# Attention of a hybrid decoder trunk: masked choice, maximum and exponential taken in the accumulator bank, sink added apart, two groups' outputs joined, keys split wider

## The chip, the cores and the metric

The kernel runs on one core of one Trainium2 chip. The metric is the device time of one execution, in microseconds (us). The kernel before takes 2112.53 us, the median of three runs between 2110.27 and 2112.72. The core has a TensorE (PE, matmuls; its weight loads are listed as PEld), a VectorE (DVE), a ScalarE (ACT), a GpSimd (POOL), a SyncE (SP) that issues the transfers here, and eight accumulator banks (PSUM) of 128 partitions by 512 fp32 values that the matmuls write.

## The reference

A trunk of two layers over 1024 tokens of width 1024. Layer 0 mixes tokens by a causal convolution module. Layer 1 mixes them by attention over a sliding window of 128 tokens, with 16 query heads, 4 key and value heads (groups of 4 heads share one), and one learned sink per head, all from one K and V computed at the start of layer 1. After each mixer come a layer norm, a squared-ReLU MLP, a second layer norm and a gated embedding.

What the change touches is the attention:

```
def swa_sink_attention(x, w_q, sinks, w_o, kk, vv, cos, sin):
    q = partial_rope((x @ w_q).reshape(B, T, N_HEADS, HEAD_DIM), cos, sin)
    scores = jnp.einsum("bnqkgd,bnskd->bnkgqs", q, kk) * (1.0 / math.sqrt(HEAD_DIM))
    scores = jnp.where(mask, scores, -jnp.inf)
    lse = jnp.logaddexp(jax.nn.logsumexp(scores, axis=-1, keepdims=True), sink)
    probs = jnp.exp(scores - lse).astype(vv.dtype)
    out = jnp.einsum("bnkgqs,bnskd->bnqkgd", probs, vv)
    return out.reshape(B, T, N_HEADS * HEAD_DIM) @ w_o
```

The queries are taken in 8 blocks of 128. A block sees 256 keys (the previous block and its own), of which the mask leaves 128 for each query: key s of the own block if s is not later than the query, else key s of the previous block. So for each query and each s from 0 to 127 exactly one of two scores counts, and the kernel chooses it (the masked choice). The first block has no previous one.

## The kernel before, in words

**How it is written and ordered.** The program does not write instructions for the engines directly. It notes them, with the tiles that they read and write, in a recorder; a planner (`schedule`) then lays all of them out in time with a cost for each operation, always taking the ready operation that comes first in program order, and issues each engine's instructions in the order that it found. On the chip each engine works through its own list in that order and waits at each instruction for what it needs. Because PE has matmuls of independent work in its list (the projection of later queries, for one), the planner can place those where attention's own matmuls are not ready yet. All instructions are issued from one line (L485), so the profile tells them apart by tile names.

**Tiles and slots.** Each kind of tile has a number of slots (`SLOTS`) that are given out in program order: `ps` 6 accumulator banks and `tr` 2, `t` 5 work tiles of 128x512, `z` 4, `g` 4, `X`, `A`, `B`, `E` for larger stores, and so on. `move(a, b)` takes one slot of kind a when it is free and makes it one of kind b. The trace names a slot by its first kind, so a bank called `ps` or `tr` in a row may serve as `sc` or `pv`. A dependency on a bank is on the whole bank, for readers too: two instructions that use one bank come one after the other.

**fp32 from two halves.** An fp32 operand is split into a high half (ACT copies it, rounded) and a rest (DVE subtracts): `split`. A product then takes three matmuls (high x high, high x rest, rest x high).

**Attention, keys and values** (`attention`). The K and V projection runs for tokens 512 to 1023 and then for 0 to 511, four blocks at a time, each block in its own bank. For each block, ACT copies V out, `rope` turns K, PE transposes K's two 128x128 pieces, and for each of the four groups ACT writes the scaled high half and DVE the rest, 64x128 each, into `kT` (64 partitions of high halves above 64 of rests, so that one matmul contracts both). Two key blocks that lie in different halves are copied side by side into `k34`.

**Attention, queries.** Then `sc` gets two of the banks and `pv` one. For gp = 0 and 1 (two groups each) and n = 0 to 7 (query blocks): 24 matmuls of 512 columns project one block's 8 heads into one `ps` bank; `rope` turns them (ACT copies, DVE multiplies and adds); POOL lays each head down twice (for the two halves of `kT`). For each of the two groups `scores` is called, and `values` for the group that came two before it.

- `scores`: 4 transposes and a split give the queries. For each pair of heads, 4 matmuls of 256 columns (128 for n = 0) fill a bank `sc`; ACT copies the previous block's scores to the SBUF tile `s`, and DVE's copy_predicated puts the own block's scores over them where the mask says so. A column of `s` beside the 128 holds the sink, put there by POOL. Once both pairs are in, one DVE reduce over 4 x 129 gives the negated maxima, four ACT exponentials over 129 columns give the weights and their sums with the sink's own term in it, DVE takes the reciprocals, and POOL scales the four heads.
- `values`: 4 transposes of the weights, a split, masked copies by POOL, and 4 matmuls of 512 columns (2 for n = 0) into the bank `pv`, whose upper 64 partitions hold the sum's second part. Heads stand in pairs: for the even and the odd heads apart, ACT copies 64x256 and DVE adds 64x256, into a tile of 128x256; a split into the final tiles follows for each group.

Where the result of group gp goes is fixed: gp = 0 into `att`, gp = 1 into the `xT` tiles that the output projection (`mix_out`) reads as its left operand.

Of the kernel before, what the change touches and what calls it, by code (L numbers as in the profile page):

```python
# [10 lines left out]
F32 = mybir.dt.float32  # L11
F32R = mybir.dt.float32r
AF = mybir.ActivationFunctionType
ALU = mybir.AluOpType
# [503 lines left out]
class Emit:  # L518
# [1383 lines left out]
    def attention(self):  # L1902
# [5 lines left out]
        o = 256 + NT * 32  # L1908
        self.sink = ac[:, o : o + NH]
        nc.sync.dma_start(self.sink, d["sinks"].to_broadcast([P, NH]))  # L1910
        self.products, self.turned = nc.tile("zz", (P, 1024)), 0

        kT = {(g, p): self.sb("B", F32R) for p in range(2) for g in range(4)}
# [8 lines left out]
        for tg in (range(4, 8), range(0, 4)):  # L1922
            nc.slack = WORK_SLACK
            for k in range(4 if tg[0] else 0):
                self.work("w_o", k, "X")
            nc.slack = 0.0
            for ps, t in zip(self.tok_group(tg, us, each=2), tg):
                nc.scalar.copy(vf[t // 2][:, t % 2 * 256 : (t % 2 + 1) * 256], ps[:, 256:512])
                kf = self.sb("t")[:, 0:256]
                self.rope(ps[:, 0:256], kf, t, 4)  # L1930

                pt = self.transpose4([kf[:, j * P : (j + 1) * P] for j in range(2)])
                cols = slice(t % 4 * P, (t % 4 + 1) * P)
                for g in range(4):
                    hi, lo = (kT[g, t // 4][r, cols] for r in ROWS)
                    src = pt[ROWS[g % 2], g // 2 * P : (g // 2 + 1) * P]
                    nc.scalar.activation(hi, src, AF.Identity, scale=HD ** -0.5)
                    nc.vector.scalar_tensor_tensor(
                        out=lo, in0=src, scalar=HD ** -0.5, in1=hi.bitcast(F32), op0=ALU.mult, op1=ALU.subtract
                    )  # L1940
                if t in (3, 4):
                    for g in range(4):
                        nc.scalar.copy(k34[:, g, t - 3, :], kT[g, t // 4][:, cols].bitcast(F32))
        ws.done(4)
        self.kT, self.k34 = kT, k34

        for a, b in (("ps", "sc"), ("ps", "sc"), ("ps", "pv"), ("bo", "v"), ("bo", "v"), ("z", "v")):
            nc.move(a, b)
        att = [self.pair("XE"[t // 4], F32R) for t in range(NT)]
        pend = []  # L1950
        for gp in range(2):
            us = ws.get(4)
            for n in range(NT):
                ps = self.tok_group([n], us)[0]

                q1 = self.sb("t")
                self.rope(ps, q1, n, 8)
                qf = [self.sb("t") for gl in range(2)]
                for gl in range(2):
                    src = q1[:, gl * 256 : (gl + 1) * 256].rearrange("p (h e) -> p h e", e=HD)  # L1960
                    nc.gpsimd.tensor_copy(
                        qf[gl].rearrange("p (h r e) -> p h r e", r=2, e=HD), src.unsqueeze(2).to_broadcast([P, 4, 2, HD])
                    )

                col = n % 2 * 256 + gp * P
                own = vf[n // 2][:, col : col + P].rearrange("p (g e) -> p g e", g=2)
                if n == 0:
                    vd = [self.value_forms(own, q1 if gp == 0 else None)]
                else:
                    if n > 1:  # L1970
                        vd = [self.value_forms(last, q1 if n < 3 and gp == 0 else None)]
                    df = self.sb("t")[:, 0:P].rearrange("p (g e) -> p g e", g=2)
                    nc.vector.tensor_tensor(out=df, in0=own, in1=last, op=ALU.subtract)
                    vd = [vd[0], self.value_forms(df, q1 if n < 3 and gp == 0 else None)]
                last = own
                for gl in range(2):
                    if gp == 0:
                        dst = [a.rearrange("p (k t) -> p k t", k=4)[:, 2 * gl : 2 * gl + 2, :] for a in att[n]]
                    else:
                        dst = [x[:, 2 * gl : 2 * gl + 2, n % 4 * P : (n % 4 + 1) * P] for x in self.xT[1, n // 4]]  # L1980
                    p = self.scores(n, 2 * gp + gl, qf[gl])
                    pend.append((p, gl, vd, dst))
                    if len(pend) > 2:
                        self.values(*pend.pop(0))
            ws.done(4)
        for p in pend:
            self.values(*p)
        nc.move("mid", "raw")
        for a, b in (("ps", "sc"), ("ps", "sc"), ("ps", "pv"), ("bo", "v"), ("bo", "v"), ("z", "v")):
            nc.move(b, a)  # L1990

        self.x = []
# [24 lines left out]
    def scores(self, n, g, qf):  # L2017

        nc = self.nc
        nb = min(n, 1) + 1  # L2020
        hs = slice(4 * g, 4 * g + 4)
        pq = self.transpose4(self.blocks(qf))
        qT = [self.sb("g", F32R) for j in range(2)]
        self.split(pq, *qT)
        sm = self.small(16)
        nm, su = (sm[:, 4 * i : 4 * i + 4] for i in range(2))
        if n == 4:
            ks = self.k34[:, g].rearrange("p b t -> p (b t)")
        else:
            o = (n % 4 + 1 - nb) * P  # L2030
            ks = self.kT[g, n // 4][:, o : o + nb * P]

        s = nc.tile("z", (P, 4 * SC)).rearrange("p (h s) -> p h s", h=4)
        with nc.after(qf) if n == 0 else contextlib.nullcontext():
            nc.gpsimd.tensor_copy(s[:, :, P], self.sink[:, hs])
            if n == 0:
                nc.gpsimd.memset(s[:, :, 0:P], NEG)
        for jj in range(2):
            ps = self.ps("sc").rearrange("p (a b) -> p a b", a=2)
            for j in range(2):  # L2040
                qs = slice((2 * jj + j) * P, (2 * jj + j + 1) * P)
                nc.tensor.matmul(ps[:, j, 0 : nb * P], qT[0][:, qs], ks, start=True, stop=False)
                nc.tensor.matmul(ps[:, j, 0 : nb * P], qT[1][:, qs], ks, start=False, stop=True)
            dst = s[:, 2 * jj : 2 * jj + 2, 0:P]
            if n:
                nc.scalar.copy(dst, ps[:, :, 0:P])
            nc.vector.copy_predicated(
                out=dst, mask=self.own.bitcast(mybir.dt.int32).unsqueeze(1).to_broadcast([P, 2, P]),
                data=ps[:, :, (nb - 1) * P : nb * P],
            )  # L2050
        nc.vector.reduce_max(out=nm, in_=s[:, :, 0 : P + 1], axis=mybir.AxisListType.X, negate=True)
        for h in range(4):
            nc.scalar.activation(
                s[:, h, 0 : P + 1], s[:, h, 0 : P + 1], AF.Exp, bias=nm[:, h : h + 1], scale=1.0,
                accum_out=su[:, h : h + 1],
            )
        nc.vector.reciprocal(su, su)
        for h in range(4):
            nc.gpsimd.tensor_scalar(
                out=s[:, h, 0:P], in0=s[:, h, 0:P], scalar1=su[:, h : h + 1], scalar2=0.0,  # L2060
                op0=ALU.mult, op1=ALU.add,
            )
        return s

    def values(self, s, gl, vd, dst):

        nc = self.nc
        pp = self.transpose4([s[:, h, 0:P] for h in range(4)])
        tr = []
        for k, v in enumerate(vd):  # L2070
            pT = [self.sb("A", F32R) for j in range(2)]
            if k == 0:
                self.split(pp, *pT)
                full = pT
            else:
                for a, b in zip(pT, full):
                    self.own_keys(a, b)
            v = v[:, gl].rearrange("p s e -> p (s e)")
            tr += [(v[:, 0:P], pT[0]), (v[:, HD : HD + P], pT[1])]
        po = self.ps("pv")  # L2080
        for i, (l, r) in enumerate(tr):
            nc.tensor.matmul(po, l, r, start=i == 0, stop=i == len(tr) - 1)
        pv = po.rearrange("p (a e t) -> p a e t", a=2, e=2)
        o = self.sb("t")[:, 0:256].rearrange("p (a t) -> p a t", a=2)
        for e in range(2):
            r = slice(e * HD, (e + 1) * HD)
            nc.scalar.copy(o[r], pv[0:HD, :, e, :])
            nc.vector.tensor_tensor(out=o[r], in0=o[r], in1=pv[HD:P, :, e, :], op=ALU.add)
        self.split(o, *dst)

    def own_keys(self, dst, src):

# [60 lines left out]
def layout(a):  # L2153
    c = np.ascontiguousarray

    def tokmov(w):
        k = w.shape[0] // P
        n = w.shape[1] // HT
        return c(w.reshape(k // 2, 2, P, n, HT).transpose(3, 0, 2, 1, 4).reshape(n, k // 2, P, 1024))
# [58 lines left out]
    r["w_o"] = tokmov(np.asarray(a["attn_w_o"])[0])  # L2218
# [23 lines left out]
```

## Time and profile before

| what | value |
|---|---|
| median of the runs (lowest, highest) | 2112.53 us (2110.27, 2112.72) |
| span of the profiled execution, first to last instruction | 2106.6 us |
| PE busy over the span | 2094.4 us (99%), 9912 matmuls |
| DVE, ACT, POOL busy over the span | 1724.8, 1232.9, 320.7 us |
| in the 150 us from 1150 to 1300 (the query loop): PE, DVE, ACT, POOL busy | 149.86, 130.56, 131.78, 97.25 us |

The profiled execution's own time is known by its span, 2106.6 us; the runs are timed from outside it and stand 5.9 us above (2112.53 less 2106.6), for what lies before the first and behind the last instruction. A row of a group reads: line, engine, operation, output tile and inputs, shapes, count, then busy time and the mean duration of one in ns, then the time that the engine stood idle just before these and what ended it. The K and V projection lies from about 1100 to 1131 us, the query loop from there to about 1315.

### The profile page before, as it was taken

What the parts mean: (1) busy time and instruction counts of PE and PEld (TensorE: products, weight loads), DVE (VectorE), ACT (ScalarE), POOL (GpSimd) and SP (SyncE); (2) the same over time, 40 slices, a digit from 0 to 9 for tenths busy, and PEclk for the clock granted to TensorE, in tenths of its full rate; (3) what the DMA queues carried; (4) which work ended last, traced back from release to release, by engine and by line L of the source; (5) the groups of instructions that cost most, each with busy time, mean ns of one, the idle gap of its engine ahead of it and who ended that gap; (6) DMA issues with size and microseconds to landing.
All of it is one profiled execution on the core that took longest, in us unless ns stands there. A gap on an engine that the chain in (4) does not pass through costs nothing.

```text
span 2106.6 us, 29589 instructions
## 1 busy us (share of the span) xinstructions
PE 2094.4 (99%) x9912; PEld 1742.3 (83%) x9912; DVE 1724.8 (82%) x2724; ACT 1232.9 (59%) x2326; POOL 320.7 (15%) x548
## 2 busy tenths in 40 slices
PE   9999999999999999999999999999999999999999
PEld 7888888888888888888888888888888888888877
DVE  8999789987876879877976888699787778888688
ACT  6776754766655533345656988367666663333374
POOL 0533114000000000002121666140000000000040
PEclk9999999999999999999999999999999999999999
DMA  6669954788786757564486113677878786575635
GB/s 225 196 203 294 302 188 155 279 270 289 255 286 209 264 174 242 187 196 150 172 308 225 61 41 117 223 235 257 277 257 283 256 284 198 180 245 168 237 117 198
DMA packets 215385, 458.51 MB, mean 218 GB/s; under 512 B 21824, under 2 KB 52288, under 8 KB 215232
## 3 DMA queue, kind: packets, MB, share of 16 engines
q1 hardware_dynamic: 215232, 456.62, 64.7%
q8 instruction: 78, 1.28, 0.2%
q14 instruction: 75, 0.61, 0.1%
HBM read 311.04 MB, written 145.49 MB: 217 GB/s over the span
## 4 chain that ended last, share of the span: by engine, by line
PE 93%; DMA 2%; DVE 2%; ACT 1%; issue 1%; POOL 1%; SPq 0%; DVEq 0%; POOLq 0%; ACTq 0%
PE ps L485 73%; PE tr L485 20%; ACT z L485 1%; POOL sm L485 1%; DMA wh<-gate_t 0%; DMA gate_low_t<-xh 0%; DMA form<-t 0%; DVE g L485 0%; DMA z<-in_w_dw_dram 0%; DMA gate_low_b<-xl 0%; DVE t L485 0%; DVE z L485 0%; SPq L485 0%; DMA X<-in_xT_dram 0%; DMA wl<-form 0%
## 5 line engine op out<-in xcount | busy, mean ns | idle before, releaser
L485 PE MATMUL ps<-xh 128*128 128x512 f32 x636 | 247.4, 389 | 0.0
L485 PE MATMUL ps<-xl,xh 128*128 128x512 f32 x636 | 247.4, 389 | 0.0
L485 PE MATMUL ps<-xh,xl 128*128 128x512 f32 x636 | 247.4, 389 | 0.0
L485 POOL TENSOR_SCALAR sm<-sm 128x1 f32<-128x1 f32 x72 | 27.1, 378 | 1371.4 <-DVE E L485 607.3
L485 PE MATMUL ps<-xh,wl 128*128 128x512 f32 x472 | 184.5, 391 | 0.1
L485 PE MATMUL ps<-xl,wh 128*128 128x512 f32 x472 | 184.2, 391 | 0.2 <-DVE xl L485 0.2
L485 PE MATMUL ps<-xh,wh 128*128 128x512 f32 x472 | 183.6, 391 | 0.0
L485 ACT CAST wh<-raw 128x1024 fp32r<-128x1024 f32 (+2 forms) x134 | 120.0, 897 | 88.1 <-PE ps L485 60.7
L485 PE MATMUL ps<-wh,xh 128*128 128x512 f32 x404 | 160.5, 399 | 3.5 <-DMA wh<-gate_t 1.2
L485 PE MATMUL ps<-wl,xh 128*128 128x512 f32 x404 | 161.0, 399 | 0.0
L485 PE MATMUL ps<-wh,xl 128*128 128x512 f32 x404 | 160.8, 398 | 0.0
L485 ACT CAST xh<-wh 128x1024 fp32r<-128x1024 f32 x76 | 79.7, 1049 | 119.6 <-PE ps L485 74.1
L485 PEld LDWEIGHTS ps<-xl,xh 128*128 128x128 f32 x636 | 119.4, 188 | 24.9
L485 PEld LDWEIGHTS ps<-xh,xl 128*128 128x128 f32 x636 | 119.4, 188 | 24.7
L485 PEld LDWEIGHTS ps<-xh 128*128 128x128 f32 x636 | 119.4, 188 | 24.6
L485 DVE TENSOR_TENSOR wl<-raw,wh 128x1024 fp32r<-128x1024 f32 (+2 forms) x100 | 98.1, 982 | 48.1 <-ACT wh L485 43.7
L485 ACT CAST wh<-g 128x512 fp32r<-128x512 f32 x136 | 81.3, 619 | 96.0 <-PE ps L485 59.1
L485 DVE TENSOR_TENSOR wl<-g,wh 128x512 fp32r<-128x512 f32 x136 | 91.1, 691 | 41.6 <-ACT wh L485 41.5
L485 DVE TENSOR_TENSOR xl<-wh,xh 128x1024 fp32r<-128x1024 f32 x76 | 92.8, 1221 | 19.0 <-ACT xh L485 18.7
L485 ACT ACTIVATE t<-t 128x512 f32<-128x512 f32 x144 | 91.1, 632 | 26.0 <-DVE t L485 24.3
L485 PEld LDWEIGHTS ps<-xh,wh 128*128 128x128 f32 x472 | 89.0, 188 | 18.5 <-ACT xh L485 0.4
L485 PEld LDWEIGHTS ps<-xl,wh 128*128 128x128 f32 x472 | 88.6, 188 | 18.8 <-DVE xl L485 0.9
(442 smaller groups left out, 5732.0 us busy)
## 6 DMA issues: line engine op xcount, KB each, us to landing
wh<-hid SPq DMA_DIRECT2D x78, 512.0 KB, 4.2
raw<-in_w_up_dram SPq DMA_DIRECT2D x68, 512.0 KB, 4.3
wl<-in_w_down_dram SPq DMA_DIRECT2D x58, 512.0 KB, 4.9
hid<-zz SPq DMA_DIRECT2D x96, 256.0 KB, 4.6
hid<-t SPq DMA_DIRECT2D x64, 256.0 KB, 4.6
z<-in_w_dw_dram SPq DMA_DIRECT2D x56, 288.0 KB, 4.0
raw<-hid SPq DMA_DIRECT2D x30, 512.0 KB, 4.0
hid<-z SPq DMA_DIRECT2D x36, 256.0 KB, 4.8
```

The source lines that it names most:

```text
L485: getattr(getattr(nc, o.eng), o.name)(*a, **k)
```

## The change

In `attention`:

- A second small tile `less` holds the negated sinks, made by one POOL instruction.
- For keys, four blocks are turned first, each into a half of a `t` tile. Then, for each of the two pieces, four transposes fill one bank, and ACT and DVE split 64x512 at a time (all four blocks of a group at once). The copies into `k34` stand behind it.
- `sc` gets three banks, so `ps` is left with two.
- The tiles that a result goes to are chosen for two groups at a time.

In `scores`:

- The scores stay in the bank. For n = 0, DVE first fills the previous block's place in the bank with a large negative number; the matmuls always write the last columns. copy_predicated chooses within the bank, a DVE reduce over 2 x 128 takes the maxima of the pair in the bank, a small DVE instruction negates them and takes the minimum with `less`, and two ACT exponentials read the bank and write `s`. This is done for each pair of heads.
- The sink's term is worked out apart, for the four heads: POOL adds sink and negated maximum, ACT takes the exponential, POOL adds it to the sums.
- ACT's copy, the sink column, POOL's fill for n = 0 and the 129th column are gone.

In `values`:

- The result of a group is one ACT copy 64x512 and one DVE add 64x512, into the lower 64 partitions of a `t` tile for the first and the upper 64 for the second group; one split of 128x512 follows for both. The order of heads that this gives is met by a change of the rows of `w_o` in `layout`, outside the timed program.

```diff
+        self.less = ac[:, o + NH : o + 2 * NH]
+        nc.gpsimd.tensor_scalar(out=self.less, in0=self.sink, scalar1=-1.0, scalar2=0.0, op0=ALU.mult, op1=ALU.add)
...
+            turned = []
             for ps, t in zip(self.tok_group(tg, us, each=2), tg):
                 nc.scalar.copy(vf[t // 2][:, t % 2 * 256 : (t % 2 + 1) * 256], ps[:, 256:512])
-                kf = self.sb("t")[:, 0:256]
-                self.rope(ps[:, 0:256], kf, t, 4)
...
-                        out=lo, in0=src, scalar=HD ** -0.5, in1=hi.bitcast(F32), op0=ALU.mult, op1=ALU.subtract
...
+                if t % 2 == 0:
+                    kf = self.sb("t")
+                turned.append(kf[:, t % 2 * 256 : (t % 2 + 1) * 256])
+                self.rope(ps[:, 0:256], turned[-1], t, 4)
+            h = tg[0] // 4
+            for j in range(2):
+                pt = self.transpose4([v[:, j * P : (j + 1) * P] for v in turned])
+                for e in range(2):
+                    hi, lo = (kT[2 * j + e, h][r] for r in ROWS)
+                    nc.scalar.activation(hi, pt[ROWS[e]], AF.Identity, scale=HD ** -0.5)
                     nc.vector.scalar_tensor_tensor(
+                        out=lo, in0=pt[ROWS[e]], scalar=HD ** -0.5, in1=hi.bitcast(F32), op0=ALU.mult, op1=ALU.subtract
                     )
...
-        for a, b in (("ps", "sc"), ("ps", "sc"), ("ps", "pv"), ("bo", "v"), ("bo", "v"), ("z", "v")):
+        for a, b in (("ps", "sc"), ("ps", "sc"), ("ps", "sc"), ("ps", "pv"), ("bo", "v"), ("bo", "v"), ("z", "v")):
...
-        nm, su = (sm[:, 4 * i : 4 * i + 4] for i in range(2))
+        nm, su, ex = (sm[:, 4 * i : 4 * i + 4] for i in range(3))
...
-        with nc.after(qf) if n == 0 else contextlib.nullcontext():
-            nc.gpsimd.tensor_copy(s[:, :, P], self.sink[:, hs])
-            if n == 0:
-                nc.gpsimd.memset(s[:, :, 0:P], NEG)
         for jj in range(2):
+            pair = slice(2 * jj, 2 * jj + 2)
             ps = self.ps("sc").rearrange("p (a b) -> p a b", a=2)
+            if n == 0:
+                nc.vector.memset(ps[:, :, 0:P], NEG)
             for j in range(2):
                 qs = slice((2 * jj + j) * P, (2 * jj + j + 1) * P)
-                nc.tensor.matmul(ps[:, j, 0 : nb * P], qT[0][:, qs], ks, start=True, stop=False)
-                nc.tensor.matmul(ps[:, j, 0 : nb * P], qT[1][:, qs], ks, start=False, stop=True)
-            dst = s[:, 2 * jj : 2 * jj + 2, 0:P]
-            if n:
-                nc.scalar.copy(dst, ps[:, :, 0:P])
+                to = ps[:, j, (2 - nb) * P : 2 * P]
+                nc.tensor.matmul(to, qT[0][:, qs], ks, start=True, stop=False)
+                nc.tensor.matmul(to, qT[1][:, qs], ks, start=False, stop=True)
+            both = ps[:, :, 0:P]
             nc.vector.copy_predicated(
...
-        nc.vector.reduce_max(out=nm, in_=s[:, :, 0 : P + 1], axis=mybir.AxisListType.X, negate=True)
-        for h in range(4):
-            nc.scalar.activation(
-                s[:, h, 0 : P + 1], s[:, h, 0 : P + 1], AF.Exp, bias=nm[:, h : h + 1], scale=1.0,
...
+            nc.vector.reduce_max(out=ex[:, pair], in_=both, axis=mybir.AxisListType.X)
+            nc.vector.scalar_tensor_tensor(
+                out=nm[:, pair], in0=ex[:, pair], scalar=-1.0, in1=self.less[:, 4 * g + 2 * jj : 4 * g + 2 * jj + 2],
+                op0=ALU.mult, op1=ALU.min,
             )
+            for h in range(2 * jj, 2 * jj + 2):
+                nc.scalar.activation(
+                    s[:, h], ps[:, h - 2 * jj, 0:P], AF.Exp, bias=nm[:, h : h + 1], scale=1.0,
+                    accum_out=su[:, h : h + 1],
+                )
+        nc.gpsimd.tensor_tensor(out=ex, in0=nm, in1=self.sink[:, hs], op=ALU.add)
+        nc.scalar.activation(ex, ex, AF.Exp)
+        nc.gpsimd.tensor_tensor(out=su, in0=su, in1=ex, op=ALU.add)
         nc.vector.reciprocal(su, su)
...
-        pv = po.rearrange("p (a e t) -> p a e t", a=2, e=2)
-        o = self.sb("t")[:, 0:256].rearrange("p (a t) -> p a t", a=2)
-        for e in range(2):
-            r = slice(e * HD, (e + 1) * HD)
-            nc.scalar.copy(o[r], pv[0:HD, :, e, :])
-            nc.vector.tensor_tensor(out=o[r], in0=o[r], in1=pv[HD:P, :, e, :], op=ALU.add)
-        self.split(o, *dst)
+        if gl == 0:
+            self.joint = self.sb("t")
+        o = self.joint
+        r = ROWS[gl]
+        nc.scalar.copy(o[r], po[0:HD])
+        nc.vector.tensor_tensor(out=o[r], in0=o[r], in1=po[HD:P], op=ALU.add)
+        if gl == 1:
+            self.split(o.rearrange("p (k t) -> p k t", k=4), *dst)
```

More of the change, by code (lines that the diff above doesn't have):

```diff
@@ L1926, in attention @@
             nc.slack = 0.0
+            turned = []
             for ps, t in zip(self.tok_group(tg, us, each=2), tg):
                 nc.scalar.copy(vf[t // 2][:, t % 2 * 256 : (t % 2 + 1) * 256], ps[:, 256:512])
-                kf = self.sb("t")[:, 0:256]
-                self.rope(ps[:, 0:256], kf, t, 4)
[L1932 to L1937, printed above, removed]
+                if t % 2 == 0:
[8 more added lines that the diff above has]
+                    nc.scalar.activation(hi, pt[ROWS[e]], AF.Identity, scale=HD ** -0.5)
                     nc.vector.scalar_tensor_tensor(
-                        out=lo, in0=src, scalar=HD ** -0.5, in1=hi.bitcast(F32), op0=ALU.mult, op1=ALU.subtract
+                        out=lo, in0=pt[ROWS[e]], scalar=HD ** -0.5, in1=hi.bitcast(F32), op0=ALU.mult, op1=ALU.subtract
                     )
-                if t in (3, 4):
-                    for g in range(4):
-                        nc.scalar.copy(k34[:, g, t - 3, :], kT[g, t // 4][:, cols].bitcast(F32))
+            for g in range(4):
+                cols = slice(0, P) if h else slice(3 * P, 4 * P)
+                nc.scalar.copy(k34[:, g, h, :], kT[g, h][:, cols].bitcast(F32))
         ws.done(4)
         self.kT, self.k34 = kT, k34
-        for a, b in (("ps", "sc"), ("ps", "sc"), ("ps", "pv"), ("bo", "v"), ("bo", "v"), ("z", "v")):
+        for a, b in (("ps", "sc"), ("ps", "sc"), ("ps", "sc"), ("ps", "pv"), ("bo", "v"), ("bo", "v"), ("z", "v")):
             nc.move(a, b)
@@ L1975, in attention @@
                 last = own
+                if gp == 0:
+                    dst = [a.rearrange("p (k t) -> p k t", k=4) for a in att[n]]
+                else:
+                    dst = [x[:, :, n % 4 * P : (n % 4 + 1) * P] for x in self.xT[1, n // 4]]
                 for gl in range(2):
[L1977 to L1980, printed above, removed]
                     p = self.scores(n, 2 * gp + gl, qf[gl])
@@ L1988, in attention @@
         nc.move("mid", "raw")
-        for a, b in (("ps", "sc"), ("ps", "sc"), ("ps", "pv"), ("bo", "v"), ("bo", "v"), ("z", "v")):
+        for a, b in (("ps", "sc"), ("ps", "sc"), ("ps", "sc"), ("ps", "pv"), ("bo", "v"), ("bo", "v"), ("z", "v")):
             nc.move(b, a)
@@ L2031, in scores @@
             ks = self.kT[g, n // 4][:, o : o + nb * P]
-        s = nc.tile("z", (P, 4 * SC)).rearrange("p (h s) -> p h s", h=4)
-        with nc.after(qf) if n == 0 else contextlib.nullcontext():
-            nc.gpsimd.tensor_copy(s[:, :, P], self.sink[:, hs])
+        s = nc.tile("z", (P, 4 * SC))[:, 0 : 4 * P].rearrange("p (h s) -> p h s", h=4)
+        for jj in range(2):
+            pair = slice(2 * jj, 2 * jj + 2)
+            ps = self.ps("sc").rearrange("p (a b) -> p a b", a=2)
             if n == 0:
-                nc.gpsimd.memset(s[:, :, 0:P], NEG)
@@ L2038, in scores @@
-        for jj in range(2):
-            ps = self.ps("sc").rearrange("p (a b) -> p a b", a=2)
+                nc.vector.memset(ps[:, :, 0:P], NEG)
             for j in range(2):
                 qs = slice((2 * jj + j) * P, (2 * jj + j + 1) * P)
-                nc.tensor.matmul(ps[:, j, 0 : nb * P], qT[0][:, qs], ks, start=True, stop=False)
-                nc.tensor.matmul(ps[:, j, 0 : nb * P], qT[1][:, qs], ks, start=False, stop=True)
-            dst = s[:, 2 * jj : 2 * jj + 2, 0:P]
-            if n:
-                nc.scalar.copy(dst, ps[:, :, 0:P])
+                to = ps[:, j, (2 - nb) * P : 2 * P]
@@ L2047, in scores @@
+                nc.tensor.matmul(to, qT[0][:, qs], ks, start=True, stop=False)
+                nc.tensor.matmul(to, qT[1][:, qs], ks, start=False, stop=True)
+            both = ps[:, :, 0:P]
             nc.vector.copy_predicated(
-                out=dst, mask=self.own.bitcast(mybir.dt.int32).unsqueeze(1).to_broadcast([P, 2, P]),
-                data=ps[:, :, (nb - 1) * P : nb * P],
-            )
-        nc.vector.reduce_max(out=nm, in_=s[:, :, 0 : P + 1], axis=mybir.AxisListType.X, negate=True)
@@ L2052, in scores @@
-        for h in range(4):
-            nc.scalar.activation(
-                s[:, h, 0 : P + 1], s[:, h, 0 : P + 1], AF.Exp, bias=nm[:, h : h + 1], scale=1.0,
-                accum_out=su[:, h : h + 1],
-            )
+                out=both, mask=self.own.bitcast(mybir.dt.int32).unsqueeze(1).to_broadcast([P, 2, P]),
+                data=ps[:, :, P : 2 * P],
+            )
+            nc.vector.reduce_max(out=ex[:, pair], in_=both, axis=mybir.AxisListType.X)
+            nc.vector.scalar_tensor_tensor(
+                out=nm[:, pair], in0=ex[:, pair], scalar=-1.0, in1=self.less[:, 4 * g + 2 * jj : 4 * g + 2 * jj + 2],
+                op0=ALU.mult, op1=ALU.min,
+            )
@@ L2059, in scores @@
             nc.gpsimd.tensor_scalar(
-                out=s[:, h, 0:P], in0=s[:, h, 0:P], scalar1=su[:, h : h + 1], scalar2=0.0,
+                out=s[:, h], in0=s[:, h], scalar1=su[:, h : h + 1], scalar2=0.0,
                 op0=ALU.mult, op1=ALU.add,
@@ L2217, in layout @@
     r["w_q"] = tokmov(np.asarray(a["attn_w_q"])[0])
-    r["w_o"] = tokmov(np.asarray(a["attn_w_o"])[0])
+    heads = np.arange(NH).reshape(2, 2, 4).transpose(0, 2, 1)
+    rows = (heads[..., None] * HD + np.arange(HD)).ravel()
+    r["w_o"] = tokmov(np.asarray(a["attn_w_o"])[0][rows])
     r["sinks"] = c(np.asarray(a["attn_sinks"]))
```

## The prediction

> **What bounds the kernel now.** I read the page's busy times first, then its chain of waits, for the engine that sets the end.
>
> ```profile
> PE 2094.4 (99%) x9912; PEld 1742.3 (83%) x9912; DVE 1724.8 (82%) x2724; ACT 1232.9 (59%) x2326; POOL 320.7 (15%) x548
> ...
> PE 93%; DMA 2%; DVE 2%; ACT 1%; issue 1%; POOL 1%; SPq 0%; DVEq 0%; POOLq 0%; ACTq 0%
> ```
>
> PE is busy 99% and is 93% of the chain. All the rest together has 2106.6 - 2094.4 = 12 us in which PE visibly stands, and the change touches only one stage. So the second view is the table by stretches of that stage, the query loop (columns: window, its length, then busy us and instructions of PE, PEld, DVE, ACT and POOL, granted clock, DMA share, GB/s).
>
> ```profile
> 1150.00:1200.00 50.00, 49.90 (x289) 42.13 (x288) 43.00 (x105) 43.40 (x158) 31.08 (x77) 1.00 0.04 12
> 1200.00:1250.00 50.00, 49.96 (x289) 41.81 (x287) 43.79 (x107) 44.15 (x148) 33.57 (x82) 1.00 0.28 96
> 1250.00:1300.00 50.00, 50.00 (x286) 41.73 (x285) 43.76 (x107) 44.23 (x147) 32.60 (x79) 1.00 0.22 64
> ```
>
> The clock is full (1.00). DVE is busy 130.56 of 150 us (87%), ACT 131.78 (88%), POOL 97.25 (65%): two engines are near their end, yet PE loses only 0.14 us visibly. Since the ends of matmuls are modelled, I count how much PE work lies in these 150 us. Three stretches without a wait give the spacing of matmuls; the first is from the chain in order of time (start, length, what), the others are from the timeline.
>
> ```profile
> 488.07 2.72 PE tr L485 x12
> ...
> 1150.24 0.99 PE L485 MATMUL ps<-B,g 128*128 128x256 f32 x7
> ...
> 1144.52 0.60 PE L485 MATMUL ps<-ident,t 128*128 128x128 f32 x4
> ```
>
> 512 columns: 2.72/12 = 0.227 us. 256 columns: the last of the seven takes 0.28 to its end, so (0.99 - 0.28)/6 = 0.118. A transpose: (0.60 - 0.27)/3 = 0.110. One query block is 24 matmuls of the projection and 8 of the values (512), 16 of the scores (256) and 16 transposes: 64 instructions, 32 x 0.227 + 16 x 0.118 + 16 x 0.110 = 10.9 us. The three windows hold 289 + 289 + 286 = 864 = 13.5 blocks, or 147.2 us of work in 150 us. **The slack of PE is 2.8 us in 150, or 3.3 us over the 16 blocks (175 us)**; matmul records that are missing would make it less. What the slack waits for is told by the chain of waits between 1060 and 1340 us:
>
> ```profile
> by line: PE ps L485 70.9%; PE tr L485 27.3%; ACT z L485 0.7%; ACT t L485 0.3%; DVE g L485 0.2%; DVE X L485 0.2%; ACT g L485 0.2%; issue 0.2%; DVE z L485 0.1%
> ```
>
> 1.8% of 280 us is off PE, 5.0 us; ACT has 1.2% of it, 3.4 us (`z` are the copied scores and the exponentials, `t` the results' copies), DVE 0.5%, 1.4 us.
>
> **The change part by part.** PE first: per block it has the same 64 instructions after as before, and the keys have the same 16 transposes, now four to a bank. Nothing is taken off the engine that sets the end, so the terms below count only where they change how long PE waits. Groups of instructions from 1090 to 1320 us, forms kept apart (count, busy us, mean ns, idle before):
>
> ```profile
> L485 ACT ACTIVATE z<-z,sm 128x129 f32<-128x129 f32 x128 | 51.6, 405 | 3.6 <-DVE sm L485 3.1
> L485 DVE COPY_PREDICATED z<-cst,ps 128x256 f32<-128x256 int32 x64 | 28.3, 445 | 5.2 <-ACT z L485 3.8 <-POOL t L485 0.3 <-PE ps L485 0.2
> L485 DVE TENSOR_TENSOR t<-t,ps 64x256 f32<-64x256 f32 x60 | 25.4, 424 | 5.1 <-ACT t L485 3.0
> L485 DVE TENSOR_REDUCE sm<-z 128x4 f32<-128x516 f32 x32 | 22.0, 686 | 0.8
> L485 ACT COPY t<-ps 64x256 f32<-64x256 f32 x60 | 21.9, 365 | 4.6 <-PE ps L485 3.6
> L485 ACT COPY z<-ps 128x256 f32<-128x256 f32 x56 | 20.7, 369 | 4.7 <-PE ps L485 3.9 <-POOL z L485 0.5
> L485 DVE TENSOR_TENSOR g<-ps,g 128x512 fp32r<-128x512 f32 x22 | 14.9, 684 | 1.2 <-ACT g L485 0.7
> L485 DVE TENSOR_TENSOR X<-X,X 128x512 fp32r<-128x512 f32 x20 | 14.6, 742 | 2.8 <-ACT X L485 2.5
> L485 ACT CAST g<-ps 128x512 fp32r<-128x512 f32 x22 | 12.7, 582 | 2.0 <-PE ps L485 1.9
> L485 ACT CAST X<-X 128x512 fp32r<-128x512 f32 x17 | 10.5, 620 | 2.4 <-DMA w_q<-X 2.4
> L485 DVE SCALAR_TENSOR_TENSOR B<-ps,B 64x128 fp32r<-64x128 f32 x24 | 6.8, 288 | 6.5 <-ACT B L485 6.2
> L485 ACT ACTIVATE B<-ps 64x128 fp32r<-64x128 f32 x24 | 6.5, 272 | 2.4 <-DVE B L485 2.1
> L485 DVE RECIPROCAL sm<-sm 128x4 f32<-128x4 f32 x32 | 5.5, 173 | 4.0 <-ACT z L485 3.5
> L485 DVE TENSOR_TENSOR E<-t,E 128x256 fp32r<-128x256 f32 x8 | 4.0, 504 | 0.1
> L485 ACT CAST E<-t 128x256 fp32r<-128x256 f32 x8 | 3.2, 402 | 0.0
> ```
>
> *ACT, per block.* The score copies go: 4 x 0.369 = -1.48. The results: before 4 x 0.365 + 2 x 0.402 = 2.26, after 2 copies of 64x512 at 0.58 (as a 512-column read of a bank) and one split of 0.62 = 1.78, so -0.48. The sink's exponential is new, 2 x 0.21 by the row below: +0.41. The exponentials now read a bank; a 512-column cast takes 582 ns from a bank and 620 from SBUF, so between 0 and 8 x 0.04 = -0.3; I take 0. Sum -1.55 of 0.88 x 10.9 = 9.6 us: ACT falls to about 74%.
>
> *DVE, per block.* From 64x256 (424) to 128x512 (684) it is 1.02 ns an element. The maxima: 2 x 0.686 = 1.37 before; after, 4 of 256 elements at 686 - 260 x 1.02 = 421 ns = 1.68, so +0.31. The minimum with `less` has no row; its bounds are the reciprocal (173) and the small three-operand row below (219); 4 x 0.2 = +0.8. copy_predicated writes a bank instead of SBUF, which no row shows: its bounds are 445 - 38 (the cast's difference) and 742 (the longest row of 512 columns); I take 445 as for the same shape, +0. The results: 4 x 0.424 + 2 x 0.504 = 2.70 before, 2 x 0.684 + 0.742 = 2.11 after, -0.59. Sum +0.52 on 0.87 x 10.9 = 9.5: DVE rises to 10.0 of 10.9 us, **92%**. The new fills for n = 0 are 8 in all, under 0.445 each, behind the whole projection of that block.
>
> The Trainium skill speaks against reading the bank more often: "VectorE: DVE Perf Modes", section "Rules for kernel authors", advises a copy to SBUF first when many operations follow on a matmul's output, and its errata section charges a source in PSUM 62 cycles (at 0.96 GHz, 65 ns) more than one in SBUF. By that the 64 reduces would cost an estimated 4.1 us more of DVE. The rows disagree: 684 ns from a bank, 742 from SBUF for 128x512, so I leave it out.
>
> *POOL, per block.* Rows of the whole trace, by engine and form:
>
> ```profile
> L485 DVE SCALAR_TENSOR_TENSOR sm<-sm,sm 128x1 f32<-128x1 f32 x24 | 5.2, 219 | 6.1 <-POOL sm L485 5.4
> ...
> L485 ACT ACTIVATE sm<-mhalf 128x1 f32<-128x1 f32 x1 | 0.2, 207 | 0.0
> ...
> L485 POOL TENSOR_TENSOR sm<-sm,mhalf 128x1 f32<-128x1 f32 x40 | 25.9, 650 | 3.1
> L485 POOL COPY z<-cst 128x4 f32<-128x4 f32 x32 | 6.9, 215 | 50.5 <-DVE xl L485 31.9 <-PE ps L485 10.5 <-PE tr L485 8.1
> ```
>
> Four small sums come, each between 0.215 and 0.650 (I take 0.3, nearer the copy, since the 650 is a power), and two copies of 0.215 go: +0.8 on 7.1 of 10.9 us, 72% (2.2 us and 85% at the upper bound). The first of the two sums, the exponential and the second stand ahead of the reciprocal and lengthen a group's chain by some 1 us; the weights' transposes come two groups later, and two groups are 10.9 us of PE work, which hides it.
>
> *Keys.* 32 ACT and 32 DVE instructions of 272 and 288 ns become 8 of 0.58 and 8 of 0.68: -4.1 and -3.8 us, in a stretch where PE has projections. The first key is ready later, by the blocks that it now waits for, but it isn't needed before the first queries are projected and turned.
>
> *Banks.* `ps` keeps two instead of three, and the first query block gets the bank of the third key block, not the second's. Timeline, that bank drained (called `tr`) and the first projection:
>
> ```profile
> 1128.46 0.37 ACT L485 COPY A<-tr 128x256 f32<-128x256 f32 x1 [1.36 <-PE tr L485]
> ...
> 1129.14 0.29 DVE L485 TENSOR_TENSOR zz<-tr,cst 128x128 f32<-128x128 f32 x1 [0.91 <-ACT t L485]
> ...
> 1131.56 0.48 PE L485 MATMUL tr<-wh,xh 128*128 128x512 f32 x1
> ```
>
> It is free at 1129.43, 2 us before the projection starts: nothing. In the loop a bank is drained in about 1.3 us (ACT's copy, DVE's product, two signals), while the other bank's projection has 24 x 0.227 = 5.4 us of matmuls: hidden, 1.3 us a block if that cover went. The third `sc` bank pays for its longer use: copy_predicated 0.45, reduce 0.42, minimum 0.2, two exponentials 0.8 and some 0.8 of signals are about 2.7 us of every 10.9/4 x 3 = 8.2.
>
> **The sum.** On the critical engine nothing. Of ACT's 3.4 us on the chain I take half, since the next to be late is DVE, which has more to do: -1.7 us (bounds 0 and -3.4). Span 2106.6 - 1.7 = 2104.9; the runs' median stands 5.9 us above the span, so **2110.8 us**, own range 2108.5 to 2112.5. A change under 0.2%, 4.2 us, can't be told from none here; this is less, and above the stage's 3.3 us of slack there is next to nothing to win.
>
> **The rivals.**
>
> *A, ACT's relief buys nothing:* PE's list is full, the waits pass from ACT to DVE at the same length. 2112.5 us. For it: DVE's 87% before; against it: ACT is named more than twice as often on the chain.
>
> *B, all of the slack comes back:* the whole 5.0 us off PE in the chain, 2107.5. For it: ACT at 74% and a third bank; against it: DVE has its own 1.4 us there, and the count of instructions gives 3.3, not 5.0.
>
> *C, the DVE chain becomes the bound, slower.* Now copy_predicated, reduce and minimum follow one another on DVE, each on the one before, eight such steps a block. Timeline rows, first a product and the sum that needs it, then two instructions that don't need each other:
>
> ```profile
> 1123.70 0.29 DVE L485 TENSOR_TENSOR zz<-ps,cst 128x128 f32<-128x128 f32 x1 [1.33 <-ACT t L485]
> ...
> 1124.10 0.29 DVE L485 TENSOR_TENSOR t<-zz 128x32 f32<-128x32 f32 x2
> ...
> 1191.66 0.43 DVE L485 COPY_PREDICATED z<-cst,ps 128x256 f32<-128x256 int32 x1
> ...
> 1191.98 0.28 DVE L485 TENSOR_TENSOR v<-A,v 128x128 fp32r<-128x128 f32 x1
> ```
>
> The first pair lies 0.11 us apart, the second overlaps by 0.11: a dependent step costs 0.22 us more where the planner puts nothing between. Eight are 1.76 us a block, DVE's free time is 10.9 - 10.0 = 0.9. From half of them unfilled PE has to wait; at three quarters it is (1.32 - 0.9) x 16 = 7 us, 2119.5, all bare 14 us, 2126. For it: 92%; against it: the list of DVE is laid out with other work ready at nearly any time, and today's 87% cost PE 3.3 us.
>
> *D, two banks are too few:* the projection can't run ahead, 1.3 us exposed a block, 16 x 1.3 = 21 us, 2133. Against it: the 5.4 us of cover.
>
> **How the numbers follow.** The forecast 0.50, A 0.18, B 0.13, C 0.16, D 0.03. The forecast and A are within 0.2%: 0.68. B is faster by more: 0.13. C and D are slower: 0.19. The range goes from just under B (2107.3) to 2119, the lighter part of C; D, C's heavier part and a little below B, near 0.15, are left out.
>
> **What would show it.** The steps hold if the query loop keeps 10.9 to 11.1 us a block (some 864 PE instructions in 150 us), ACT there falls to about three quarters, DVE rises to about 92%, the reduces take near 420 ns, and the groups `z<-ps` (copy) are gone. C would show as fewer PE instructions in 150 us with DVE in the chain's shares, D as PE idle before projections behind ACT's `t` copies. The prediction is wrong if PE's instruction count changes, or if the loop's length moves by over 4 us either way.

## The result and the profile after

The changed kernel takes 2135.85 us (median of 4 runs, 2135.48 to 2136.59) against 2111.72 us of the kernel before (4 runs): a ratio of 1.0113, 95% interval 1.0101 to 1.0125. It is 24 us **slower**; the forecast was 2110.8 with a range up to 2119.

From the page of the kernel after: busy times, and the chain of waits by engine.

```profile
PE 2108.2 (99%) x9912; PEld 1746.7 (82%) x9912; DVE 1725.2 (81%) x2757; ACT 1209.6 (57%) x2230; POOL 323.3 (15%) x576
...
PE 90%; DVE 3%; DMA 3%; ACT 2%; POOL 1%; issue 1%; SPq 0%; DVEq 0%; ACTq 0%; POOLq 0%
```

PE has the same 9912 matmuls. Its visible idle time is 2134.4 - 2108.2 = 26.2 us instead of 12, the chain leaves it for 10% instead of 7%. ACT has 23 us less to do, DVE the same. The stretches of the query loop, kernel after:

```profile
1150.00:1200.00 50.00, 45.54 (x243) 37.06 (x244) 37.36 (x102) 32.51 (x117) 28.70 (x76) 0.97 0.03 11
1200.00:1250.00 50.00, 47.04 (x256) 37.41 (x256) 38.34 (x107) 34.91 (x110) 30.84 (x78) 1.00 0.29 96
1250.00:1300.00 50.00, 46.74 (x249) 37.43 (x249) 39.46 (x110) 31.82 (x110) 28.55 (x74) 0.97 0.03 12
```

748 PE instructions in 150 us, where there were 864: 11.7 blocks, 12.8 us each instead of 11.1. And **no engine is near its end**: DVE is busy 115 of 150 us (77%; 87% before), ACT 99 (66%; 88%), POOL 88 (59%; 65%). So this is no overloaded engine; PE stands in a chain of short waits. What PE waits for, from 1130 to 1345 us (us in total, times, longest):

```profile
PE ps L485 <- DVE zz L485: 7.2, 12, 1.2
PE ps L485 <- DVE ps L485: 2.5, 1, 2.5
PE ps L485 <- POOL z L485: 1.7, 3, 1.0
```

`zz` is the product of the turning (`rope`): DVE reads the projected queries from their bank and is the last to read them. The first row says that the projection of the next block stands until that bank is free. One block of the timeline shows it (start, length, engine):

```profile
1214.54 0.39 PE L485 MATMUL ps<-wh,xl 128*128 128x512 f32 x1
...
1215.20 1.37 PE L485 MATMUL ps<-ident,z 128*128 128x128 f32 x4 [0.26 <-POOL z L485]
...
1215.77 0.58 ACT L485 COPY t<-ps 128x512 f32<-128x512 f32 x1
...
1216.39 0.42 DVE L485 TENSOR_TENSOR zz<-ps,cst 128x256 f32<-128x256 f32 x1 [0.71 <-ACT t L485]
...
1216.86 0.50 PE L485 MATMUL ps<-wh,xh 128*128 128x512 f32 x1 [0.30 <-DVE zz L485]
```

The last projection matmul starts at 1214.54; ACT copies it at 1215.77, behind two exponentials and the sink's, DVE multiplies until 1216.81, and 0.05 us later the next projection starts. From start to start that is 2.32 us, in which PE has one matmul (0.227) and four transposes (0.44): 1.65 us are lost. The transposes in between take a stretched 1.37 us because they follow POOL, which scales the weights one head at a time. The same reckoning for all 16 blocks, each from its own timeline (the last one to the first matmul of the output projection), gives 0.4 to 3.4 us a block and **22.0 us in all**; in the kernel before it gives 0.2 us in all. It counts all time that PE loses between two projections, whatever else it also waited for.

The longest of the 16, 3.4 us from 1149.6, shows how the drain stretches. ACT had just begun an ACT_TABLE_LOAD, the only one from 1095 to 1350 us (count, busy us, mean ns, idle before),

```profile
L485 ACT ACT_TABLE_LOAD x1 | 1.3, 1283 | 2.8 <-DVE sm L485 2.8
```

and took five exponentials and one of a sink behind it, before it copied the bank at 1152.56. PE's wait of 2.5 us for `DVE ps`, the second row above, lies in the same time: the scores of an n = 0 waited for DVE's fill, and the fill for a bank that those exponentials still read. In the kernel with two `sc` banks (below) ACT loads the table at the same place and a fill waits 1.6 us, and PE has no wait at all from 1148 to 1156 us: it goes on projecting into the second bank.

### The profile page after: what moved, and what is told of

Read it like the earlier page. It is cut to its first block, busy times and chain, and to the rows that moved or that the text cites. A ratio compares the mean times of both kernels' runs of the same rounds, so it can differ in the third digit from the quotient of the medians.

```text
span 2134.4 us, 29551 instructions
## 1 busy us (share of the span) xinstructions
PE 2108.2 (99%) x9912; PEld 1746.7 (82%) x9912; DVE 1725.2 (81%) x2757; ACT 1209.6 (57%) x2230; POOL 323.3 (15%) x576
## 4 chain that ended last, share of the span: by engine, by line
PE 90%; DVE 3%; DMA 3%; ACT 2%; POOL 1%; issue 1%; SPq 0%; DVEq 0%; ACTq 0%; POOLq 0%
PE ps L485 73%; PE tr L485 17%; ACT z L485 1%; DMA wh<-gate_t 1%; DMA hid<-zz 1%; DVE sm L485 1%; POOL sm L485 1%; DVE t L485 0%; ACT t L485 0%; DMA t<-proj 0%; DVE ps L485 0%; DMA raw<-in_w_kv_dram 0%; DVE zz L485 0%; DVE wl L485 0%; DVE A L485 0%
## 5 line engine op out<-in xcount | busy, mean ns | idle before, releaser
L485 PE MATMUL ps<-wh,xh 128*128 128x512 f32 x464 | 187.7, 406 | 11.4 <-DVE zz L485 7.2
L485 PE MATMUL ps<-xl,wh 128*128 128x512 f32 x492 | 192.3, 391 | 0.2 <-DVE xl L485 0.2
L485 PE MATMUL ps<-xh,wl 128*128 128x512 f32 x492 | 192.1, 391 | 0.0
L485 PE MATMUL ps<-xh,wh 128*128 128x512 f32 x492 | 191.8, 392 | 0.2 <-ACT v L485 0.2
L485 PE MATMUL ps<-wl,xh 128*128 128x512 f32 x464 | 186.1, 401 | 0.0
L485 PE MATMUL ps<-wh,xl 128*128 128x512 f32 x464 | 185.9, 401 | 0.0
L485 PEld LDWEIGHTS ps<-wh,xh 128*128 128x128 f32 x464 | 88.0, 190 | 32.4 <-DVE zz L485 10.4
L485 PEld LDWEIGHTS ps<-xh,wl 128*128 128x128 f32 x492 | 92.5, 188 | 19.6 <-DMA wl<-form 0.4
```

The costliest lines, as they stand in the source:

```text
L485: getattr(getattr(nc, o.eng), o.name)(*a, **k)
```

## The experiments

All times are compared with runs of the kernel before that were taken beside them: median 2111.88 us for the first four, 2111.90 for the others. In the cuts of code, "..." stands for the rest of a line or for lines left out; where a line of moves is changed, the line behind the loop that gives the banks back is changed in the same way.

**Where the banks really stand.** After the result I counted the banks in the program's own moves, which I had not done: between the start and the attention there are `ps` to `tr` one at line 1274, three back at 1519, three to `tr` at 1672, two back at 1833, four to `tr` at 1869, two back at 1882. From 6 and 2 that leaves **five `ps` and three `tr`**, not six and two. So `ps` kept two for the projection before and keeps one after; the text ahead of the prediction (two left) and the prediction (two instead of three) are both one too high. The trace could have told it. Projection matmuls of one kind in the loop, first the kernel before, then the kernel after:

```profile
L485 PE MATMUL ps<-wh,xh 128*128 128x512 f32 x68 | 27.7, 407 | 0.0
...
L485 PE MATMUL tr<-wh,xh 128*128 128x512 f32 x67 | 27.2, 407 | 0.0
```

```profile
L485 PE MATMUL ps<-wh,xh 128*128 128x512 f32 x136 | 57.9, 426 | 7.3 <-DVE zz L485 7.2
...
L485 PE MATMUL tr<-wh,xh 128*128 128x512 f32 x1 | 0.4, 389 | 0.0
```

Before, half of these matmuls go to a bank named `ps` and half to one named `tr`, with no waiting. In order of time it is one block of 24 matmuls to `ps` and the next to `tr`, in turn, from 1153 us to the end of the loop: two banks. After, all blocks go to `ps`, with 7.3 us of waiting. In the two kernels with three projection banks (below) one name takes two blocks and then the other takes one, as the count of moves says.

**Two `sc` banks again**, nothing else undone.

```diff
-(("ps", "sc"), ("ps", "sc"), ("ps", "sc"), ("ps", "pv"), ...)
+(("ps", "sc"), ("ps", "sc"), ("ps", "pv"), ...)
```

> The changed kernel with `sc` back at two banks and nothing else undone. The theory that banks decide: in the planner's own list of moves the attention starts with five `ps` and three `tr`, not six and two, so the kernel before kept two banks for the projection of the queries and the changed one keeps a single one; each block's projection then waits until that bank is drained. With two again nearly all of the 24 us comes back: 2110 to 2116 us. The theory that the longer DVE chain in the bank decides (copy_predicated, reduce, minimum, then the exponentials): with fewer banks for the chain it stays at 2136 us or gets slower.

Measured: 2114.67 us, ratio 1.0011 (1.0002 to 1.0020): as expected, 21 of the 24 us come back. The rival, the longer chain on DVE, wanted this kernel as slow or slower.

**The third `sc` bank alone, in the kernel before.** The same line, the other way round.

> The kernel before with the third `sc` bank alone and nothing else of the change. If banks decide, it has one bank for the projection and loses at least what the changed kernel lost: 2130 to 2150 us. If the DVE chain decides, it stays within 3 us of the kernel before, 2109 to 2115 us, since its scores, results and keys are the old ones.

Measured: 2161.3 us, ratio 1.0240 (1.0223 to 1.0258): 49 us slower, more than the bank theory's upper end. PE's waits in the loop:

```profile
PE ps L485 <- DVE zz L485: 11.3, 13, 2.9
PE tr L485 <- POOL z L485: 7.4, 4, 3.3
PE ps L485 <- POOL z L485: 6.1, 4, 2.4
```

The same wait is at the top, and longer (2.9 us at most, 1.2 in the changed kernel). The old scores with one bank are thus worse off than the new ones with one bank by 25 us. The traces tell where most of it goes. By the reckoning above, this kernel loses 37.5 us over its 16 blocks, 15.5 more than the changed one. The difference lies in how long the full bank waits for ACT's copy: from the end of the block's last matmul to the copy's start it is 1.46 us on average here and 0.49 in the changed kernel, while the copy (0.57 and 0.59) and the product (0.42 and 0.42) take the same. The likely reason is ACT's list, which still has the score copies and twice as many copies of results in it. The rest fits the clock: the granted clock over a run is 0.991 to 0.997 here, the lowest in the longest run, and 0.997 to 0.999 in the changed kernel; by the middle values, 0.9935 of 2160 us and 0.998 of 2135, an estimate is 14 us of missing clock against 4, and 15.5 and 10 make the 25.

**The third `sc` bank taken from `tr`.** Three `sc` as in the changed kernel, two `ps`, two `tr`.

```diff
-(("ps", "sc"), ("ps", "sc"), ("ps", "sc"), ("ps", "pv"), ...)
+(("tr", "sc"), ("ps", "sc"), ("ps", "sc"), ("ps", "pv"), ...)
```

> The changed kernel with three `sc` banks as it is, but the third taken from `tr` (two left) instead of from `ps` (two left). If the projection's single bank decides, 2110 to 2117 us, though the chain in the bank and the number of `sc` banks are those of the changed kernel. If the DVE chain or the longer use of the `sc` banks decides, 2133 to 2139 us.

Measured: 2111.07 us, ratio 0.9997 (0.9988 to 1.0007): no difference from the kernel before that can be told. This parts the number of `sc` banks and the work in them (both as in the changed kernel) from the projection's banks. Its loop:

```profile
1150.00:1200.00 50.00, 50.00 (x292) 42.53 (x291) 42.57 (x125) 38.13 (x134) 32.52 (x89) 1.00 0.04 12
1200.00:1250.00 50.00, 50.00 (x289) 42.53 (x288) 43.73 (x123) 38.29 (x129) 30.97 (x82) 1.00 0.30 96
1250.00:1300.00 50.00, 50.00 (x283) 41.50 (x282) 42.96 (x114) 37.08 (x121) 34.38 (x86) 1.00 0.27 85
```

864 PE instructions in 150 us, just as before, with ACT at 113.5 of 150 us (76%) and DVE at 129.3 (86%).

**The one bank drained sooner.** In `rope` the product reads ACT's copy `f` in SBUF instead of the bank.

```diff
-            in0=pv[:, :, 0:ROPE].unsqueeze(2).to_broadcast([P, n, 2, ROPE]), in1=table, op=ALU.mult,
+            in0=fv[:, :, 0:ROPE].unsqueeze(2).to_broadcast([P, n, 2, ROPE]), in1=table, op=ALU.mult,
```

> The changed kernel with its single projection bank, but the turning product reads ACT's copy in SBUF instead of the bank, so the bank is free after the copy alone. If the drain of the one bank is what PE waits for, some 0.5 to 0.7 us of each of 16 blocks come back, 8 to 11 us: 2125 to 2128 us. If the DVE chain decides, it stays at 2134 to 2138 us, since DVE has the same instructions.

Measured: 2128.81 us, ratio 1.0081 (1.0066 to 1.0096): 7 us back, a little less than the 8 to 11 expected. PE's first waits:

```profile
PE ps L485 <- ACT z L485: 5.7, 9, 2.2
PE ps L485 <- ACT t L485: 2.9, 5, 0.7
```

`DVE zz` is gone from PE's waits; ACT's copy (`t`) now ends the projection's wait, and a wait for the exponentials (`ACT z`), which give the `sc` banks free, stands above it. DVE has the same instructions, so it was the length of the drain, and not the amount of DVE's work, that gave the 7 us.

**Three projection banks**, in the changed kernel with two `sc` and two `tr`, and in the kernel before with two `tr`.

```diff
-(("ps", "sc"), ("ps", "sc"), ("ps", "sc"), ("ps", "pv"), ...)
+(("tr", "ps"), ("ps", "sc"), ("ps", "sc"), ("ps", "pv"), ...)
```

> The changed kernel with two `sc`, three `ps` and two `tr` banks: one bank more for the projection than the kernel before had. If the single bank was the whole loss, a third buys nothing over the second: 2111 to 2116 us, as with two `sc` and two `ps` (2114.7). If the loop is still short of projection banks, it gains 2 us or more on that.

> The kernel before with one `tr` bank made a third `ps` (three `ps`, two `sc`, one `pv`, two `tr`). If two projection banks already cover the drain, as a drain of about 2 us against 10 us of spread-out projection says, no change: 2110 to 2113 us. If the slack that PE still has in the loop comes from the projection's banks, 2107 to 2109.5 us.

Measured: 2113.47 us (ratio 1.0005, 0.9996 to 1.0014) and 2112.69 us (1.0001, 0.9992 to 1.0010). Beyond two, a bank for the projection buys nothing that can be told.

**The results joined and the keys split wider, alone**: `values`, its targets, the order of `w_o` and the key part of `attention` as in the change, `scores` and the banks as before.

```diff
+            for j in range(2):
+                pt = self.transpose4([v[:, j * P : (j + 1) * P] for v in turned])
...
+        nc.scalar.copy(o[r], po[0:HD])
+        nc.vector.tensor_tensor(out=o[r], in0=o[r], in1=po[HD:P], op=ALU.add)
+        if gl == 1:
+            self.split(o.rearrange("p (k t) -> p k t", k=4), *dst)
```

> The kernel before with the joined results and the wider key splits alone, old scores, old banks. They take ACT and DVE work off (per block about 0.5 and 0.6 us) and touch no bank. If ACT's lateness set PE's slack, as forecast, 2109 to 2111.5 us; if PE's list is full and the relief buys nothing, 2111 to 2113 us.

Measured: 2112.74 us, ratio 1.0001 (0.9992 to 1.0010). In the three windows ACT falls from 131.8 to 125.3 us and DVE from 130.6 to 123.3, and no gain of PE shows.

**The scores in the bank, alone**: `scores` and `less` as in the change, the rest and the banks (two `sc`, two `ps`) as before.

```diff
+            both = ps[:, :, 0:P]
...
+            nc.vector.reduce_max(out=ex[:, pair], in_=both, axis=mybir.AxisListType.X)
...
+                    s[:, h], ps[:, h - 2 * jj, 0:P], AF.Exp, bias=nm[:, h : h + 1], scale=1.0,
```

> The kernel before with the scores kept in the bank alone (choice, maximum, exponentials there, sink apart), old results and keys, two `sc` and two `ps` as before. The bank theory: within 0.2% of before, 2110 to 2116 us, a few us at the loop's end where the last group's longer chain has no matmuls left to hide it. If the chain in the bank is dear by itself with only two `sc` banks to hold it, 2118 us or more.

Measured: 2117.87 us, ratio 1.0027 (1.0016 to 1.0039): 6 us slower, between the two expectations. PE's weight loads wait for the exponentials that free an `sc` bank, 13 times; in the kernel with two `sc` banks and all else changed 9 times, with three `sc` hardly any more. First rows of the three, in that order:

```profile
PEld ps L485 <- ACT z L485: 5.6, 13, 1.3
```

```profile
PEld ps L485 <- ACT z L485: 2.9, 9, 0.5
```

```profile
PEld ps L485 <- ACT z L485: 0.4, 1, 0.4
```

So with the bank held through the exponentials, two `sc` banks are a little short, and the third is worth some 2.4 to 3.6 us (2113.47 or 2114.67 to 2111.07). Taken from `tr` it costs nothing that shows; taken from `ps` the kernel is 24 us slower than the one before.

## Why the prediction was wrong, step by step

- **The step that failed is "Banks".** It reads "`ps` keeps two instead of three" and hides the drain behind "the other bank's projection". There was no other bank: two became one. The cover that the step named (5.4 us of matmuls in the other bank) was gone, and the step's own price for that case, 1.3 us a block, became the result: measured, 1.4 us a block (22.0/16). That these two agree so closely is luck. The drain, from the end of a block's last matmul to the next block's first, took 1.85 us on average: the copy 0.59, the product 0.42 and the time between and behind them, 0.35, are near the price, but ACT's copy also stood 0.49 us behind other work of ACT. PE in turn filled some 0.6 us a block with transposes and scores. The price knew neither. Rival D, "two banks are too few ... 16 x 1.3 = 21 us, 2133", had the right wait (projections behind the drain) and nearly the right time (2135.85), with 0.03 of the chance, because I took the number of banks from the table of slots at the program's start, and six lines of moves stand between that table and the place where it counts. The trace before, with one block in `ps` and the next in `tr`, would have shown two banks in use.
- **C, the DVE chain, is refuted** by the kernel with the third `sc` from `tr`: the same instructions on DVE, 2111.07 us. DVE was to rise to 92%; with PE unhindered it is 86%, no more than before. Two of the signs that the prediction named for C did come, fewer PE instructions in 150 us and DVE on the chain (3% instead of 2%): with a single bank they come too, so they don't tell C from D. The durations were near: the reduce took 415 ns (421 worked out), the minimum 183 (200), copy_predicated in the bank 424 instead of 445, within its bounds:

```profile
L485 DVE COPY_PREDICATED ps<-cst,ps 128x256 f32<-128x256 int32 x64 | 26.1, 424 | 5.3 <-PE ps L485 3.9 <-ACT t L485 0.6
...
L485 DVE TENSOR_REDUCE sm<-ps 128x2 f32<-128x256 f32 x64 | 25.5, 415 | 0.2
...
L485 DVE SCALAR_TENSOR_TENSOR sm<-sm,cst 128x2 f32<-128x2 f32 x64 | 11.4, 183 | 0.2
```

What was wrong in this term is that it takes a sum of durations for busy time. The durations of DVE's instructions that start in the 150 us do add up to more, 143.6 us before and 150.3 with the third `sc` from `tr` (0.50 a block; 0.52 forecast), but the time in which DVE was busy is 130.5 and 130.3: DVE's instructions overlap, as the rows of C themselves showed (0.11 us).
- **ACT's relief was sized right and bought nothing that shows.** 76% was measured with two projection banks, 74% forecast; the exponentials read the bank in 367 ns instead of 405 (bounded at -38). But the -1.7 us for PE don't show: the third `sc` from `tr` gives -0.8 us (interval -2.5 to +1.5), the results and keys alone +0.8 (-1.7 to +2.1). That is rival A, once the banks are put right, but a gain of 1.7 us is too small for these intervals to exclude. Where banks are short the relief does count: with one projection bank the old scores take 2161.3 us and the changed kernel 2135.85, and by the reckoning above 15.5 of these 25 us are a shorter drain, with ACT sooner at the full bank.
- **The fills for n = 0** were put at nothing, "behind the whole projection of that block". With one projection bank one of them stood in PE's longest wait, 2.5 us; with two, such a fill waited 1.6 us and PE did not. So this term failed with the same step as the banks.
- **The third `sc` bank "pays for its longer use"**: right in kind, and its worth is now measured, 2.4 to 3.6 us.
- **PE's work is the same**: right, 9912 matmuls, 64 a block. The bound on the gain (3.3 us of slack) also held: no kernel here came out clearly faster than the one before.
- **The time around the span.** I put the median 5.9 us above the span, as if both came from one execution. The changed kernel's profiled execution took 2136.14 us with a span of 2134.4, 1.7 us apart. The profiled execution of before was a short one, by an estimate with the same 1.7 near 2108.3 us; so some 4 us of the 5.9 was the spread of executions, and the difference of the spans, 27.8 us, overstates that of the medians, 24.1.

What stays open: where exactly the last microsecond or two of the kernel with two `sc` go (the wait for the exponentials was seen there, but not taken away apart from the third bank), and whether the lighter work gains PE a microsecond. That ACT's shorter list is what halves the loss with one bank is read from the traces; no run takes ACT's copies away alone.

## What to carry to other kernels

Before a buffer is moved from one use to another, count what is left at that place, from the program's moves or from which buffers the trace shows in turn, not from the table at the start. The work that fills in for others needed two buffers of its own here: with one, the time from its last write to its last read came into the open every round, on an engine that looked 99% busy. And this kernel, whose critical engine was full, gained nothing that shows from lighter helpers, while it lost at once what kept it full.

## What the runs showed of the hardware

The granted clock of TensorE is 1.00 in every stretch of the loop before, and falls to 0.97 in two of three after; with two projection banks (the third `sc` from `tr`, or two `sc`) it is 1.00 in all three. Closer in, around the longest wait of the kernel after:

```profile
1148.00:1152.00 4.00, 1.96 (x11) 1.33 (x10) 2.31 (x9) 2.55 (x8) 0.20 (x1) 1.00 0.00 0
1152.00:1154.00 2.00, 0.97 (x5) 0.86 (x6) 1.26 (x6) 1.52 (x8) 1.28 (x5) 0.92 0.03 8
1154.00:1156.00 2.00, 2.00 (x8) 1.45 (x8) 0.61 (x4) 0.46 (x2) 1.65 (x4) 0.50 0.00 0
1156.00:1158.00 2.00, 2.00 (x10) 1.63 (x10) 0.87 (x2) 1.04 (x4) 0.50 (x3) 0.72 0.00 0
1158.00:1160.00 2.00, 2.00 (x16) 1.73 (x15) 1.01 (x3) 1.49 (x3) 1.25 (x4) 1.00 0.00 0
```

PE had little to do from 1150 to 1153.7 us (a wait of 2.48 us, four short matmuls, another wait), and then the clock was halved: the missing clock in these rows is 2 x (0.08 + 0.50 + 0.28) = 1.7 us, so 3.4 us at 0.50. Matmuls that follow one another in 0.227 us before do so in 0.43 in another such stretch at 1280.7:

```profile
1280.68 0.63 PE L485 MATMUL ps<-wl,xh 128*128 128x512 f32 x1
1281.11 0.63 PE L485 MATMUL ps<-wh,xl 128*128 128x512 f32 x1
```

Two such dips lie in the loop, each behind a stretch of 3 us or more with few matmuls, and none in these 150 us of the kernels with two or three projection banks; so 3.4 us of the loss go with the clock, and with the 22.0 us they make 25.4. A third, a clock of 0.83 in the 10 us from 260 (1.7 us missing), stands in code that the change doesn't touch, and some profiles of other kernels have it and some, that of the kernel before among them, don't. With it, 27.1 of the 27.8 us between the two spans are found. For such falls of the clock the Trainium skill states a rule, in "TensorE: Matmul & The Clock Gate", section "HAM oscillation — how this bites in real kernels": no idle gaps of PE above about 3.4 us. The trace agrees in kind, a clock of 0.50 after too little work, but here no single gap was that long; a stretch of 3.7 us with a wait of 2.48, four short matmuls and a wait of 0.60 in it was enough.
